# Unread matrix products in PE's queue at eleven places between stages of a two-block transformer kernel

## The chip, the cores and the metric

The kernel runs on one core of a Trainium2 chip. The metric is the device time of one execution in microseconds (us). The core's engines work side by side, each from a queue of its own: PE multiplies matrices (its weight loads are listed as PEld), DVE, ACT and POOL do the element-wise work, SP starts most transfers. PE's clock has two levels, 1.2 and 2.4 GHz; the profile shows the level that was granted as 0.50 or 1.00.

## The reference

Two transformer blocks run one after the other, each with two layers, on 512 latent tokens and 256 context tokens of width 1024 in f32. Cut to what matters here:

```
for l in range(2):                       # first block
    a = rmsnorm(h) * (1 + sc1) + sh1
    y = even_mixer(a) if l == 0 else odd_mixer(a)   # attention; output projection inside
    h = h + g1 * y
    h = h + g2 * swiglu(rmsnorm(h) * (1 + sc2) + sh2)
x = rmsnorm(h)
for i in range(2):                       # second block
    y = rwkv_pool_mixer(..) if i == 0 else na_mixer(..)
    x = layer_norm(alpha * x + g_m * y)
    x = layer_norm(alpha * x + g_f * swiglu(x * (1 + sc_f) + sh_f))
```

Each normalisation needs the mean of squares of a token over all 1024 features, and so all the output chunks of the stage before it.

## The kernel before

The residual `h` lies transposed in eight chunks of 128 features (partitions) by up to 768 tokens. A product of f32 accuracy is made of three passes (`mm3`): weights and inputs are split into a high and a low part, and high x high (L306), high x low (L308) and low x high (L310) are added in one PSUM tile (`pd` or `sc`). Weights come by SP's transfers; ACT makes the high part (L298), POOL the low one (L299). Inputs are split in the same way (ACT L509, DVE or POOL L510).

Between two stages stands a statistic, `Stat`. For each output chunk DVE adds the gated result to the residual (L574), ACT squares it, and DVE sums the squares (L181). When the last chunk is in, `finish` adds over the partitions with eight tiny PE products (L195), DVE makes the reciprocal root in a chain of small operations (`st_r`, L446 last), and PE spreads it over the partitions by f32 products of 128x128 with the identity (L453, `bcast`); with layer_norm the mean `st_m` goes the same way. Then chunk by chunk DVE normalises (L557, L558), ACT scales, and the parts are split; these are the inputs of the next stage's passes.

`by_parts` makes the last chunks of a stage in two halves of the tokens, so that the first half's statistic (`next(norm)`) runs beside the second half's passes; then `Fill(norm).drain()` does the rest. `out_proj` and `out_late` (second block, behind rwkv) and the feed-forward's last group (`ffn`) end in it. In `out_late` the context tokens are a third part, whose statistic comes ahead of these two. The mixers `even_mixer` and `odd_mixer` begin with a `prep`: the first projections, copies to SBUF by ACT (keys `ks`, values `vs`), rotary embedding on DVE and POOL, transposes of the values (`token_major`, L748), scores (L861 in the even mixer, L1085 in the odd one), softmax on DVE and ACT.

All this is written in program order, and a scheduler puts it into one queue for each engine; PE takes its queue in that order. The small PSUM tiles are named `pq`, of which there are two buffers.

Of the kernel before, what the change touches and what calls it, by code (L numbers as in the profile page):

```python
# [21 lines left out]
P = 128  # L22
D = 1024
KC = 8
NL = 512
NC_ = 256
T = NL + NC_
# [3 lines left out]
LAST = 3  # L31
# [112 lines left out]
class Stat:  # L144
# [44 lines left out]
    def finish_(self, x, z):  # L189
# [10 lines left out]
        if self.mean:  # L200
            m = k.small("st_m", 8)[:, :nb]
            q = k.small("st_q", 8)[:, :nb]
            nc.vector.tensor_scalar(m, ps[:, 8:8 + nb], 1.0 / D, None, op0=ALU.mult)
            nc.vector.tensor_tensor(out=q, in0=m, in1=m, op=ALU.mult)
            nc.vector.scalar_tensor_tensor(v, v, EPS, q, op0=ALU.add, op1=ALU.subtract)
        k.rsqrt(r, v, nb)
        if self.rt:
# [10 lines left out]
class Kern:  # L218
# [65 lines left out]
    def segs(n):  # L284
        return [(0, 512, 0)] + ([(512, n, 512)] if n > 512 else [])


    def wload(self, src, lo_eng=None):
# [243 lines left out]

    def ln_modulated(self, out, h, n, st, lname, m, sh, sc, scale, dst=None, parts=None):

# [15 lines left out]
        for y, z in parts:  # L550
            st.finish(y, z)
            if (y, z) != parts[-1]:
                yield
            r = int(y >= NL)
            for k in range(KC):
# [19 lines left out]

    def by_parts(self, ws, x, n, done, norm):

        for a, b in self.parts(n):
            for i, hl in ws:
                ps = self.pd()  # L580
                for kc in range(len(hl)):
                    self.mm3(ps, *hl[kc], x[0][kc], x[1][kc], kc == 0, kc == len(hl) - 1, [(a, b, a)])
                done(i, ps, a, b)
            if a == 0:
                next(norm, None)
        Fill(norm).drain()

# [5 lines left out]

    def out_proj(self, w, y, order, load, m, g, n, h, st, norm):

        with self.tc.tile_pool(name=self.nm("ylo"), bufs=6, reuse_waits="tile") as yp:
            self.out_proj_(w, y, order, load, m, g, n, h, st, norm, yp)

    def out_proj_(self, w, y, order, load, m, g, n, h, st, norm, yp):
        nc = self.nc  # L600
# [15 lines left out]
        for k in range(2, KC - LAST):  # L616
            done(k, self.chunk(w[k], y, n), 0, n)
        self.by_parts([(k, self.wload(w[k])) for k in range(KC - LAST, KC)], y, n, done, norm)

# [10 lines left out]

    def ffn(self, x, wg, wu, wo, h, m, g, n, st, norm, fill, parts):

# [10 lines left out]
        def down(gi, hid):  # L643
# [34 lines left out]
            if last:  # L678
                self.by_parts(late, xs, n, done, norm)

# [70 lines left out]
    def even_mixer(self, x, first):  # L751
# [8 lines left out]
        def prep(h):  # L760
# [8 lines left out]
            psk = psk or self.chunk(w[12 + h], x, T)  # L769
            nc.scalar.copy(ks, psk[:, :T])  # L770
            self.rope(ks)
            k1, klo = self.stack_k(ks, T)
# [160 lines left out]

    def values(self, ps):

# [4 lines left out]
        for pt, a, b in self.token_major(vs):  # L940
            nc.scalar.copy(v[:, a:b], pt)
        return v.rearrange("p (b d) -> p b d", d=P)

# [86 lines left out]
    def odd_mixer(self, x):  # L1030
# [19 lines left out]
        def prep(c):  # L1050
            kc = c // 4
            if c % 4 == 0:
# [3 lines left out]
                psk = psk or self.chunk(w[8 + kc], x, T)  # L1056
                nc.scalar.copy(ks, psk[:, :T])
                self.rope(ks)
                for s in range(2):
# [7 lines left out]
                yield  # L1067
                v = self.values(psv or self.chunk(w[10 + kc], x, T))
                kv[2 * kc] += (v,)
# [86 lines left out]

    def ffn_block(self, a, win, wout, l, h, m, g, n, st, norm, fill=None, parts=None):
        wi, wo = self.I[win], self.I[wout]
        self.ffn(a, lambda c: wi[l * 44 + c], lambda c: wi[l * 44 + 22 + c], lambda c: wo[l * 22 + c], h, m, g, n, st, norm, fill or Fill(), parts)

# [11 lines left out]
    def layer0(self):  # L1172
# [4 lines left out]
        with ExitStack() as es:  # L1177
# [9 lines left out]
            norm = self.rms_modulated(a, h, T, st, "norm2_g0", m, 24, 32)  # L1187
            self.out_proj(I["even_w_out"], y, [4, 5, 6, 7, 0, 1, 2, 3], load, m, 16, T, h, st, norm)
            self.dump("hm0", h, T)
        with ExitStack() as es:  # L1190
# [3 lines left out]
            norm = self.rms_modulated(b, h, T, st, "norm1_g1", job[0], 0, 8)  # L1194
            self.ffn_block(a, "ffn_w_in", "ffn_w_out", 0, h, m, 40, T, st, norm, Fill(self.ada(job, range(6))))
        self.dump("h0", h, T)
        return h, b, job

    def layer1(self, h, a, job):
        I = self.I  # L1200
        m = job[0]
        with ExitStack() as es:
# [6 lines left out]
            norm = self.rms_modulated(a, h, NL, st, "norm2_g1", m, 24, 32)  # L1209
            self.out_proj(I["odd_w_out"], y, list(range(KC)), self.load([(self.spd, 0, NL, None)]), m, 16, NL, h, st, norm)  # L1210
            self.dump("hm1", h, NL)
# [411 lines left out]
    def out_late(self, h, st, m, norm):  # L1623
# [10 lines left out]
        for k in range(KC - LAST):  # L1634
# [7 lines left out]
            if k == NORMAT:  # L1642
                next(norm)
        self.by_parts([(k, wl(k)) for k in range(KC - LAST, KC)], xs, NL, done, norm)

# [237 lines left out]
    def second(self, h, st, job):  # L1883
# [3 lines left out]
        with self.es2 as es0:  # L1887
# [9 lines left out]
            with ExitStack() as es:  # L1897
# [4 lines left out]
                st, b = self.stat(T, True), self.pairs()  # L1902
                norm = self.ln_modulated(b, h, T, st, "01", job[0], 0, 8, ALPHA)
                self.ffn_block(a, "ffn_w13", "ffn_w2", 0, h, m, 40, T, st, norm, Fill(self.ada(job, range(6))), parts)
            m = job[0]
            with ExitStack() as es:
# [8 lines left out]
                norm = self.ln_modulated(a, h, NL, st, "10", m, 24, 32, ALPHA)  # L1915
                self.out_proj(I["od_w_out"], y, list(range(KC)), self.load([(self.spd, 0, NL, None)]), m, 16, NL, h, st, norm)
                self.dump("xm1", h, NL)
# [215 lines left out]
```

## Time and profile before

| | |
|---|---|
| median of 3 runs | 4023.65 us (4017.19 to 4030.66) |
| the profiled execution | 4027.45 us, of which 4025.6 are the span from first to last instruction |
| mean granted clock of PE | 0.943 |
| PE busy | 3673.8 us, 91% of the span |
| DVE, ACT, POOL busy | 2253.0, 1347.9, 1348.5 us (56%, 33%, 33%) |

Busy shares are means over stages with different limits; what a place between stages is worth is read from the timeline there: what PE waits for, how long, and what it does next. In the rows that are shown further down, the value in square brackets is the idle time of the engine before the instruction, with what ended it. A row `x4` stands for four records in a row; an f32 product of 128x128 makes two of them. Matmuls overlap, so that the price of one is the distance between starts rather than its own length.

### The profile page before, as it was taken

The numbers are of one execution on the slowest core, as the hardware profiler recorded it, in microseconds if no ns is written. First come the engines' busy times: TensorE is split into PE (matmuls) and PEld (weight loads), VectorE is DVE, ScalarE is ACT, GpSimd is POOL, SyncE is SP. The second block draws the span as 40 slices with busy tenths as digits, with TensorE's granted clock in tenths as the row PEclk, the third lists the DMA queues.
The fourth block names the chain that finished last, engine by engine and source line by source line (L and its number), as shares of the span: only waits on it lengthen the run. The fifth ranks groups of instructions, "written<-read, shape, count | busy, mean of one in ns | idle before, by whom it ended". The sixth has DMA issues, their size and how long they took to land. (4 is left out here: it accounts for less than half of the span.)

```text
span 4025.6 us, 57375 instructions
## 1 busy us (share of the span) xinstructions
PE 3673.8 (91%) x22809; PEld 3183.3 (79%) x22809; DVE 2253.0 (56%) x4289; ACT 1347.9 (33%) x2337; POOL 1348.5 (33%) x798
## 2 busy tenths in 40 slices
PE   6989999999789899999877879699999899989997
PEld 4777799999677778877765667599999777778886
DVE  4884554333776677746777564755444654364225
ACT  5542212112466222234333222331111365543223
POOL 2112332222312444432221125552222542245443
PEclk9999999999899999989987779899999899999998
DMA  5124133333101255424445677223334222122331
GB/s 195 38 90 158 56 110 126 121 119 117 49 27 53 89 176 175 158 82 127 128 138 175 200 204 265 82 64 122 119 121 127 72 63 64 57 74 79 100 95 58
DMA packets 263003, 450.19 MB, mean 112 GB/s; under 512 B 63504, under 2 KB 168592, under 8 KB 259664
## 3 DMA queue, kind: packets, MB, share of 16 engines
q1 hardware_dynamic: 257536, 424.50, 33.6%
q10 hardware_dynamic: 5200, 22.02, 1.7%
q8 instruction: 180, 2.95, 0.3%
q14 instruction: 87, 0.71, 0.1%
HBM read 383.02 MB, written 63.44 MB: 111 GB/s over the span
## 5 line engine op out<-in xcount | busy, mean ns | idle before, releaser
L299 POOL TENSOR_TENSOR wlo<-wraw,whi 128x1024 fp32r<-128x1024 f32 (+2 forms) x406 | 941.5, 2321 | 1944.0 <-ACT whi L298 1820.2
L306 PE MATMUL pd<-s,whi 128*128 128x384 f32 (+2 forms) x3481 | 1050.7, 354 | 38.1 <-ACT s L509 9.5
L310 PE MATMUL pd<-s,wlo 128*128 128x384 f32 (+2 forms) x3481 | 1045.0, 351 | 1.6 <-POOL wlo L299 1.6
L308 PE MATMUL pd<-s,whi 128*128 128x384 f32 (+2 forms) x3421 | 1034.0, 352 | 12.3 <-DVE s L510 5.2
L298 ACT CAST whi<-wraw 128x1024 fp32r<-128x1024 f32 (+2 forms) x414 | 406.0, 982 | 1589.9 <-PE pd L308 899.6
L306 PEld LDWEIGHTS pd<-s,whi 128*128 128x128 f32 x3481 | 630.9, 191 | 104.7 <-issue 14.6
L308 PEld LDWEIGHTS pd<-s,whi 128*128 128x128 f32 x3421 | 622.3, 191 | 69.8 <-DVE s L510 7.6
L310 PEld LDWEIGHTS pd<-s,wlo 128*128 128x128 f32 x3481 | 632.1, 191 | 56.2 <-POOL wlo L299 3.5
L372 DVE SCALAR_TENSOR_TENSOR junk<-wraw,cond 128x1024 bf16<-128x1024 f32 x160 | 275.3, 1721 | 383.9 <-DMA wraw<-in_ada_w 383.7
L574 DVE SCALAR_TENSOR_TENSOR h<-pd,mod,h 128x256 f32<-128x256 f32 (+3 forms) x407 | 206.3, 547 | 187.7 <-PE pd L310 186.2
L696 DVE TENSOR_TENSOR s<-s,pd 128x768 f32<-128x768 f32 (+1 forms) x80 | 65.3, 817 | 289.2 <-PE pd L310 283.2
L306 PE MATMUL pd<-hid,whi 128*128 128x384 f32 (+2 forms) x624 | 192.7, 346 | 4.7 <-DVE h L574 4.2
L308 PE MATMUL pd<-hid,whi 128*128 128x384 f32 (+2 forms) x624 | 191.6, 344 | 0.9 <-DVE hid L335 0.9
L310 PE MATMUL pd<-hid,wlo 128*128 128x384 f32 (+2 forms) x624 | 191.0, 343 | 0.0
L966 DVE TENSOR_REDUCE negm<-sc 128x1 f32<-128x512 f32 (+1 forms) x128 | 96.2, 754 | 117.1 <-PE sc L1147 106.1
L372 DVE SCALAR_TENSOR_TENSOR wraw<-wraw,cond 128x1024 f32<-128x1024 f32 x96 | 133.2, 1388 | 4.0
L306 PEld LDWEIGHTS pd<-hid,whi 128*128 128x128 f32 x624 | 117.7, 192 | 15.8 <-DVE h L574 2.4
L306 PE MATMUL pd<-in,whi 128*128 128x256 f32 (+1 forms) x384 | 113.4, 362 | 14.4 <-DVE h L1240 12.4
L308 PEld LDWEIGHTS pd<-hid,whi 128*128 128x128 f32 x624 | 117.7, 192 | 9.7 <-DVE hid L335 1.3
L310 PEld LDWEIGHTS pd<-hid,wlo 128*128 128x128 f32 x624 | 117.7, 192 | 8.2
L181 DVE TENSOR_TENSOR s<-s,s 128x256 f32<-128x256 f32 (+2 forms) x106 | 101.7, 960 | 36.6 <-ACT s L180 35.0
L308 PE MATMUL pd<-in,whi 128*128 128x256 f32 (+1 forms) x384 | 115.0, 366 | 2.9 <-POOL in L510 1.9
(377 smaller groups left out, 5717.9 us busy)
## 6 DMA issues: line engine op xcount, KB each, us to landing
wraw<-in_ada_w SPq DMA_DIRECT2D x160, 512.0 KB, 3.5
wraw<-in_ffn_w SPq DMA_DIRECT2D x132, 512.0 KB, 3.6
wraw<-in_ffn_w_in SPq DMA_DIRECT2D x88, 512.0 KB, 3.6
wraw<-in_ffn_w_out SPq DMA_DIRECT2D x44, 512.0 KB, 3.5
recd<-xr SPq DMA_DIRECT2D x72, 256.0 KB, 2.9
rec<-recd ACTq DMA_DIRECT2D x12, 1536.0 KB, 7.3
rec<-recd SPq DMA_DIRECT2D x12, 1536.0 KB, 7.0
raw<-in_ada_w SPq DMA_DIRECT2D x32, 512.0 KB, 5.8
```

Of the source, the lines that this page charges most:

```text
L181: nc.vector.tensor_tensor(out=self.sq[:, a:b], in0=self.sq[:, a:b], in1=t[:, a:b], op=ALU.add)
L298: nc.scalar.copy(hi, raw)
L299: (lo_eng or nc.gpsimd).tensor_tensor(out=lo, in0=raw, in1=hi.bitcast(F32), op=ALU.subtract)
L306: nc.tensor.matmul(ps[:, o:o + b - a], lhsT=whi, rhs=xhi[:, a:b], start=start, stop=False)
L308: nc.tensor.matmul(ps[:, o:o + b - a], lhsT=whi, rhs=xlo[:, a:b], start=False, stop=False)
L310: nc.tensor.matmul(ps[:, o:o + b - a], lhsT=wlo, rhs=xhi[:, a:b], start=False, stop=stop)
L372: nc.vector.scalar_tensor_tensor(raw if r else self.junk, raw, 1.0, self.cond[r], op0=ALU.mult, op1=ALU.mult, accum_out=m[:, j, r:r + 1])
L574: nc.vector.scalar_tensor_tensor(h[k][:, x:y], ps[:, x - o:y - o], m[:, g + k, r:r + 1], h[k][:, x:y], op0=ALU.mult, op1=ALU.add)
L696: nc.vector.tensor_tensor(out=cut(sl), in0=cut(sl), in1=bank(pu), op=ALU.mult)
L966: nc.vector.tensor_reduce(nm, ps[:, base:T], axis=AX.X, op=ALU.max, negate=True)
```

## The change

A new function issues n products of the ones matrix with 128 columns of a tile into one `pq` tile; nothing reads it. Eleven places call it, with 16 to 50 products, 311 in all. Signatures on the way gain an argument. The diff, cut to its core:

```
+    def warm(self, x, n):
+        if n:
+            ps = self.pq()[:, :P]
+            for _ in range(n):
+                self.nc.tensor.matmul(ps, lhsT=self.ones, rhs=x[:, :P], start=True, stop=True)
...
@@ finish_ (st.rt: layer 1's end, ahead of rwkv)
+        if self.rt and z == self.n:
+            k.warm(self.sq[:, x:z], 16)
         k.rsqrt(r, v, nb)
...
@@ ln_modulated
             if (y, z) != parts[-1]:
                 yield
+            if y == parts[0][0]:
+                self.warm(st.r[:, y:z], warm)
...
@@ by_parts
             if a == 0:
                 next(norm, None)
+        if warm:
+            self.warm(h[ws[-1][0]][:, a:b], warm)
         Fill(norm).drain()
...
@@ even_mixer, prep
             nc.scalar.copy(ks, psk[:, :T])
+            if h == 0:
+                self.warm(ks[:, NL:], 35)
             self.rope(ks)
...
@@ values
         for pt, a, b in self.token_major(vs):
             nc.scalar.copy(v[:, a:b], pt)
+        self.warm(vs, warm)
...
@@ odd_mixer, prep
                 nc.scalar.copy(ks, psk[:, :T])
+                if c == 0:
+                    self.warm(ks[:, NL:], 25)
                 self.rope(ks)
...
-                v = self.values(psv or self.chunk(w[10 + kc], x, T))
+                v = self.values(psv or self.chunk(w[10 + kc], x, T), 0 if c else 35)
...
@@ the numbers for by_parts: first block's out_proj 20 and 20, its first feed-forward 20;
@@ second block: out_late, first feed-forward, out_proj
-        self.by_parts([(k, wl(k)) for k in range(KC - LAST, KC)], xs, NL, done, norm)
+        self.by_parts([(k, wl(k)) for k in range(KC - LAST, KC)], xs, NL, done, norm, h, 50)
...
-                norm = self.ln_modulated(b, h, T, st, "01", job[0], 0, 8, ALPHA)
+                norm = self.ln_modulated(b, h, T, st, "01", job[0], 0, 8, ALPHA, warm=35)
...
-                self.ffn_block(a, "ffn_w13", "ffn_w2", 0, h, m, 40, T, st, norm, Fill(self.ada(job, range(6))), parts)
+                self.ffn_block(a, "ffn_w13", "ffn_w2", 0, h, m, 40, T, st, norm, Fill(self.ada(job, range(6))), parts, 15)
...
-                self.out_proj(I["od_w_out"], y, list(range(KC)), self.load([(self.spd, 0, NL, None)]), m, 16, NL, h, st, norm)
+                self.out_proj(I["od_w_out"], y, list(range(KC)), self.load([(self.spd, 0, NL, None)]), m, 16, NL, h, st, norm, 40)
```

Line numbers of the changed file are some 9 to 18 higher: the products are its L295, L306/L308/L310 become L315/L317/L319, L453 becomes L462. Three places in PE's queue follow, each before and changed.

PE's queue behind `out_late`, before: the second statistic's sums and spreading, the first passes of the feed-forward (`pd_2278x`), the third sums.

```order
L195 MATMUL pq_22532<-ones_79,s_22216 128x1 x2
L195 MATMUL pq_22532<-ones_79,s_22218 128x1 x2
L453 MATMUL pq_22532<-ident_72,st_r_22538 128x128 x2
L453 MATMUL pq_22563<-ident_72,st_m_22540 128x128 x2
L306 MATMUL pd_22784<-s_22472,whi_22768 128x256
L308 MATMUL pd_22784<-s_22473,whi_22768 128x256
L310 MATMUL pd_22784<-s_22472,wlo_22769 128x256
...
L306 MATMUL pd_22786<-s_22480,whi_22780 128x256
L195 MATMUL pq_22663<-ones_79,s_22216 128x1 x2
L195 MATMUL pq_22663<-ones_79,s_22218 128x1 x2
L308 MATMUL pd_22786<-s_22481,whi_22780 128x256
```

The same place now.

```order
L195 MATMUL pq_22710<-ones_79,s_22394 128x1 x2
L195 MATMUL pq_22710<-ones_79,s_22396 128x1 x2
L462 MATMUL pq_22710<-ident_72,st_r_22716 128x128 x2
L462 MATMUL pq_22741<-ident_72,st_m_22718 128x128 x2
L295 MATMUL pq_22793<-h_21207,ones_79 128x128 x8
L195 MATMUL pq_22892<-ones_79,s_22394 128x1 x2
L195 MATMUL pq_22892<-ones_79,s_22396 128x1 x2
L295 MATMUL pq_22793<-h_21207,ones_79 128x128 x26
L462 MATMUL pq_22892<-ident_72,st_r_22898 128x128 x2
L295 MATMUL pq_22793<-h_21207,ones_79 128x128 x3
L462 MATMUL pq_22923<-ident_72,st_m_22900 128x128 x2
L295 MATMUL pq_22793<-h_21207,ones_79 128x128 x13
L315 MATMUL pd_23013<-s_22650,whi_22997 128x256
```

The 50 products have four places around the last statistic, and the feed-forward's first pass, which stood ahead of the third sums and of the third spreading, stands behind the last product. Of the 64 passes that stood ahead of the third spreading none is left there.

PE's queue at the end of block 2's first feed-forward, before: the context's spreading, the mixer's first passes, the last sums (39 passes in all stand ahead of the last spreading).

```order
L453 MATMUL pq_26957<-ident_72,st_r_26967 128x128 x4
L453 MATMUL pq_26994<-ident_72,st_m_26969 128x128 x4
L306 MATMUL pd_27312<-s_27118,whi_27296 128x512
L306 MATMUL sc_27313<-s_27118,whi_27302 128x512
L306 MATMUL sc_27314<-s_27118,whi_27308 128x512
L308 MATMUL pd_27312<-s_27119,whi_27296 128x512
L195 MATMUL pq_27178<-ones_79,s_26787 128x1 x2
L195 MATMUL pq_27178<-ones_79,s_26789 128x1 x2
L310 MATMUL pd_27312<-s_27118,wlo_27297 128x512
L308 MATMUL sc_27313<-s_27119,whi_27302 128x512
```

The same place now, down to the first half of the last spreading.

```order
L295 MATMUL pq_27343<-h_21207,ones_79 128x128 x15
L295 MATMUL pq_27359<-s_27017,ones_79 128x128 x13
L195 MATMUL pq_27459<-ones_79,s_27016 128x1 x2
L195 MATMUL pq_27459<-ones_79,s_27018 128x1 x2
L295 MATMUL pq_27359<-s_27017,ones_79 128x128 x22
L315 MATMUL pd_27593<-s_27399,whi_27577 128x512
...
L315 MATMUL sc_27595<-s_27407,whi_27589 128x512
L462 MATMUL pq_27459<-ident_72,st_r_27465 128x128 x2
```

28 products stand ahead of the last sums, 22 behind them, and of the mixer's passes 16 are left ahead of the last spreading; the three that stood ahead of the sums now follow them.

PE's queue at the odd mixer's entry, before: the last of 24 query passes (`pd_8605`), the transposes of the values, the first scores.

```order
L306 MATMUL pd_8605<-s_8302,whi_8601 128x512
L308 MATMUL pd_8605<-s_8303,whi_8601 128x512
L310 MATMUL pd_8605<-s_8302,wlo_8602 128x512
L748 MATMUL pq_8556<-ident_72,s_8553 128x128 x3
L748 MATMUL pq_8561<-ident_72,s_8553 128x128 x3
L1085 MATMUL sc_8580<-s_8541,s_8573 128x256 x2
L1048 MATMUL sc_8580<-msk_8385,identr_77 128x128
L1085 MATMUL sc_8580<-s_8542,s_8573 128x256 x2
```

The same place now: keys copied, 25 products, and so on.

```order
L295 MATMUL pq_8614<-s_8612,ones_79 128x128 x25
L315 MATMUL pd_8745<-s_8331,whi_8741 128x512
L761 MATMUL pq_8660<-ident_72,s_8657 128x128 x3
L761 MATMUL pq_8665<-ident_72,s_8657 128x128 x3
L317 MATMUL pd_8745<-s_8332,whi_8741 128x512
L295 MATMUL pq_8670<-s_8657,ones_79 128x128 x35
L1103 MATMUL sc_8720<-s_8645,s_8713 128x256 x2
L1064 MATMUL sc_8720<-msk_8463,identr_77 128x128
L1103 MATMUL sc_8720<-s_8646,s_8713 128x256 x2
L319 MATMUL pd_8745<-s_8331,wlo_8742 128x512
```

Only two of the 24 query passes (now `pd_8745`) are left ahead of the first scores; 25 products stand ahead of the transposes and 35 behind them.

## Rows read from the trace of the kernel before

**Rows 1.** The page's busy times, share of the span, instructions.

```profile
PE 3673.8 (91%) x22809; PEld 3183.3 (79%) x22809; DVE 2253.0 (56%) x4289; ACT 1347.9 (33%) x2337; POOL 1348.5 (33%) x798
```

**Rows 2.** Windows: stretch, us, PE busy (count), granted clock, DMA share, GB/s.

```profile
87.40:107.90 20.50, 16.23 (x44) 0.50 0.09 26
459.40:466.30 6.90, 6.40 (x18) 0.51 0.23 76
1070.40:1087.50 17.10, 8.43 (x31) 0.50 0.11 32
2603.00:2626.90 23.90, 11.00 (x56) 0.57 0.12 39
3193.50:3214.00 20.50, 11.40 (x37) 0.50 0.36 118
3613.40:3627.00 13.60, 7.75 (x35) 0.50 0.23 76
2700.00:2800.00 100.00, 100.00 (x579) 1.00 0.36 116
```

**Rows 3.** PE's timeline behind out_late: start, us, instruction, [idle before <- releaser].

```profile
2608.19 1.87 PE L195 MATMUL pq<-ones,s 128*128 128x1 f32 x8 [9.75 <-DVE s L181]
2616.68 1.22 PE L453 MATMUL pq<-ident,st_r 128*128 128x128 f32 x4 [6.61 <-DVE st_r L446]
2617.77 1.19 PE L453 MATMUL pq<-ident,st_m 128*128 128x128 f32 x4
2618.61 0.56 PE L306 MATMUL pd<-s,whi 128*128 128x256 f32 x1
...
2622.50 1.05 PE L195 MATMUL pq<-ones,s 128*128 128x1 f32 x8 [1.09 <-DVE s L181]
...
2631.20 0.71 PE L453 MATMUL pq<-ident,st_r 128*128 128x128 f32 x4 [0.29 <-DVE st_r L446]
...
2651.60 0.62 PE L306 MATMUL pd<-s,whi 128*128 128x512 f32 x2 [1.01 <-ACT s L691]
```

**Rows 4.** Windows of the passes into pd tiles alone, columns as in 2.

```profile
2618.60:2631.20 12.60, 10.29 (x64) 0.81 0.00 1
2632.10:2650.80 18.70, 18.48 (x152) 1.00 0.00 1
3620.90:3644.90 24.00, 21.57 (x144) 0.87 0.01 2
```

**Rows 5.** PE's timeline behind the second block's od out_proj.

```profile
3619.25 1.87 PE L195 MATMUL pq<-ones,s 128*128 128x1 f32 x8 [7.87 <-DVE s L181]
...
3628.06 0.61 PE L453 MATMUL pq<-ident,st_r 128*128 128x128 f32 x4
3628.51 0.61 PE L453 MATMUL pq<-ident,st_m 128*128 128x128 f32 x4
...
3646.83 0.50 PE L306 MATMUL pd<-s,whi 128*128 128x512 f32 x1 [2.21 <-ACT s L691]
```

**Rows 6.** PE's timeline at the end of block 2's first feed-forward.

```profile
3202.60 0.80 PE L306 MATMUL pd<-s,whi 128*128 128x512 f32 x1 [6.87 <-ACT s L509]
...
3207.07 1.70 PE L195 MATMUL pq<-ones,s 128*128 128x1 f32 x8
...
3223.10 0.71 PE L453 MATMUL pq<-ident,st_r 128*128 128x128 f32 x4 [2.91 <-DVE st_r L446]
```

**Rows 7.** PE's timeline at the odd mixer's entry.

```profile
1071.09 1.54 PE L748 MATMUL pq<-ident,s 128*128 128x128 f32 x6 [4.78 <-ACT s L938]
1078.54 0.77 PE L1085 MATMUL sc<-s,s 128*128 128x256 f32 x2 [5.90 <-DVE s L723]
```

**Rows 8.** Timeline of ACT and PE at the even mixer's entry.

```profile
82.72 0.80 ACT L770 COPY s<-sc 128x768 f32<-128x768 f32 x1
...
90.11 0.79 PE L861 MATMUL sc<-s,s 128*128 128x512 f32 x1 [6.36 <-ACT s L737]
```

**Rows 9.** PE's timeline behind block 1's first out_proj.

```profile
460.06 1.65 PE L306 MATMUL pd<-s,whi 128*128 128x512 f32 x3 [0.50 <-ACT s L509]
```

More of the change, by code (lines that the diff above doesn't have):

```diff
@@ L205, in finish_ @@
             nc.vector.scalar_tensor_tensor(v, v, EPS, q, op0=ALU.add, op1=ALU.subtract)
+        if self.rt and z == self.n:
+            k.warm(self.sq[:, x:z], 16)
         k.rsqrt(r, v, nb)
@@ L285, in segs, with warm @@
         return [(0, 512, 0)] + ([(512, n, 512)] if n > 512 else [])
+    def warm(self, x, n):
+        if n:
+            ps = self.pq()[:, :P]
+            for _ in range(n):
+                self.nc.tensor.matmul(ps, lhsT=self.ones, rhs=x[:, :P], start=True, stop=True)
     def wload(self, src, lo_eng=None):
@@ L531, in rms_modulated, with ln_modulated @@
                 self.split_part(out, k, a, x, y)
-    def ln_modulated(self, out, h, n, st, lname, m, sh, sc, scale, dst=None, parts=None):
+    def ln_modulated(self, out, h, n, st, lname, m, sh, sc, scale, dst=None, parts=None, warm=0):
         nc = self.nc
@@ L574, in residual_add, with by_parts @@
                 nc.vector.scalar_tensor_tensor(h[k][:, x:y], ps[:, x - o:y - o], m[:, g + k, r:r + 1], h[k][:, x:y], op0=ALU.mult, op1=ALU.add)
-    def by_parts(self, ws, x, n, done, norm):
+    def by_parts(self, ws, x, n, done, norm, h=None, warm=0):
         for a, b in self.parts(n):
@@ L617, in out_proj_ @@
             done(k, self.chunk(w[k], y, n), 0, n)
-        self.by_parts([(k, self.wload(w[k])) for k in range(KC - LAST, KC)], y, n, done, norm)
+        self.by_parts([(k, self.wload(w[k])) for k in range(KC - LAST, KC)], y, n, done, norm, h, warm)
     def load(self, srcs):
@@ L629, in load, with ffn @@
         return f
[L631 removed]
+    def ffn(self, x, wg, wu, wo, h, m, g, n, st, norm, fill, parts, warm):
         nc = self.nc
@@ L678, in down @@
             if last:
-                self.by_parts(late, xs, n, done, norm)
+                self.by_parts(late, xs, n, done, norm, h, warm)
         before = None
@@ L932, in lam, with values @@
         return lam
-    def values(self, ps):
+    def values(self, ps, warm=0):
         nc = self.nc
@@ L1067, in prep @@
                 yield
-                v = self.values(psv or self.chunk(w[10 + kc], x, T))
+                v = self.values(psv or self.chunk(w[10 + kc], x, T), 0 if c else 35)
                 kv[2 * kc] += (v,)
@@ L1209, in layer1 @@
             norm = self.rms_modulated(a, h, NL, st, "norm2_g1", m, 24, 32)
-            self.out_proj(I["odd_w_out"], y, list(range(KC)), self.load([(self.spd, 0, NL, None)]), m, 16, NL, h, st, norm)
+            self.out_proj(I["odd_w_out"], y, list(range(KC)), self.load([(self.spd, 0, NL, None)]), m, 16, NL, h, st, norm, 20)
             self.dump("hm1", h, NL)
@@ L1643, in out_late @@
                 next(norm)
-        self.by_parts([(k, wl(k)) for k in range(KC - LAST, KC)], xs, NL, done, norm)
+        self.by_parts([(k, wl(k)) for k in range(KC - LAST, KC)], xs, NL, done, norm, h, 50)
     def rw_invert(self, c, xls):
@@ L1915, in second @@
                 norm = self.ln_modulated(a, h, NL, st, "10", m, 24, 32, ALPHA)
-                self.out_proj(I["od_w_out"], y, list(range(KC)), self.load([(self.spd, 0, NL, None)]), m, 16, NL, h, st, norm)
+                self.out_proj(I["od_w_out"], y, list(range(KC)), self.load([(self.spd, 0, NL, None)]), m, 16, NL, h, st, norm, 40)
                 self.dump("xm1", h, NL)
```

27 lines of the change are left out of this document (18 added, 9 removed).

## The prediction

> **What bounds the kernel now.** The page's busy lines come first: TensorE (PE) computes for 3673.8 us of the 4025.6 us span [rows 1]; no other engine comes near. Next come stretches of that engine. Inside a feed-forward it is never idle: 100.00 busy in 100.00 us, granted clock 1.00 [rows 2]. There, whatever is put into its queue, or whatever useful pass is done later, lengthens the kernel one for one. The idle time lies where stages meet: the last chunk of one must be added, squared, summed, normalised and split on DVE, ACT and POOL before the next can start. At those places the granted clock has fallen to 0.50, the lower level of 1.2 GHz (one stretch holds a little more, 0.57): six stretches of 6.9 to 23.9 us each [rows 2], with PE computing in them for 16.23, 6.40, 8.43, 11.00, 11.40 and 7.75 us. So there is something to win: if that work ran at 2.4 GHz it would take half, 61.2 / 2 = 30.6 us less. Whether it is won is read from the timeline: does PE wait there for another engine, or does it already have useful passes to do?
>
> The junction behind out_late has both [rows 3]. PE waits 9.75 us for DVE's sum of squares (L181), makes the sums (L195), waits 6.61 us for the reciprocal root (st_r, L446), and spreads it (L453). But then, from 2618.61 on, it does feed-forward passes on inputs already there, while DVE does the statistics of the last part. The third sums stand at 2622.50, the third L453 is released at 2631.20. By then 64 of the 216 passes of this first group are done; 152 follow [rows 4].
>
> **What one product costs.** The added product (f32, 128x128) doesn't exist in the trace under its own name; L453 has the same shape and type, and is two records per product. Four such records take 0.45 us from 3628.06 to 3628.51 [rows 5], so a product is 0.22 us at the higher clock. At the lower one, 2617.77 to 2618.61 is 0.84 us for four [rows 3], 0.42 a product. The 311 products are thus 68 us of PE time at full clock and 131 at half. What of that lies in waits costs nothing; the rest, and passes pushed behind it, does.
>
> **Where the products stand.** The order of PE's queue shows that they aren't all in waits.
>
> Out_late, 50 products. None stands in the 9.75 us, none in the 6.61 us: the first 8 come behind the second L453, 26 behind the third L195, 3 and 13 around the third L453, and only then the first feed-forward pass. The first 34 fill DVE's statistics, 2618.6 to 2631.2: 8 x 0.42 = 3.4 us, up to the sums at 2622.50, then 26 x 0.22 = 5.7 us, done by about 2629 to 2631. So r goes out at 2631.20 as before, then 0.45, 3 products 0.66, m 0.45, 13 products 2.86: passes start near 2635.6. All 216 are still to do, at 0.12 us each (152 in 18.48 [rows 4]): 25.9 us, so 2661.5. Before, the group ended at 2650.6 (2651.60 less its idle 1.01 [rows 3]). Late by 10.9. The idle of 1.01 could take as much back. Even if the root came at once, 42 products behind the sums of 2622.50 (1.05 us) end at 2632.8, passes at 2658.7: +8, less 1 is 7. I take **+10, bounds +7 and +11**. Behind it PE is dense, so nothing returns it.
>
> Block 2, first feed-forward's end, 15 + 35 products. 28 fall into the wait of 6.87 us [rows 6]; that hides them (28 x 0.22 = 6.2 us; at 0.42, 11.8, still short of the sums near 3207). The other 22 stand behind L195 (ended near 3208.8): to 3213.6 or, slow, 3218. Then the order has 16 passes ahead of the last L453, where before it had 39. The L453 itself waits for DVE until 3223.10. So 23 passes of 512 columns (twice the 0.12 of 256, an estimate: 0.24) move behind it: 5.5 us. Waits of the mixer that follows may return some: **+4, bounds 0 and +6**.
>
> Second block's od out_proj, 40 products. The first 5 fill a little of the 7.87 us idle; 20 stand behind the sums (end near 3621.1): to 3625.5 or 3629.6. Then r, 3, m, 12 (0.45 + 0.66 + 0.45 + 2.64 = 4.2): passes start between 3629.7 and 3633.8, 144 of them [rows 4] x 0.12 = 17.3: 3647.0 to 3651.1, where before they ended at 3644.6 (3646.83 less 2.21 [rows 5]). **+4, bounds +2 and +7.** Its cold stretch is already in this: the passes that ran there at half rate are now counted at full rate.
>
> Odd mixer's entry, 25 + 35. Before, PE used the wait for 24 useful passes, idled 4.78, transposed at 1071.09, idled 5.90, and scored at 1078.54 [rows 7]. Now 25 products take the passes' place (23 passes, 5.5 us, go behind the first scores) and 35 stand behind the transposes: started near 1073.1, mixed clock, until about 1081 to 1083. Scores start 2 to 4 later; against this stands half of 8.43 busy at the lower clock, 4.2, and softmax waits. **+2.5, bounds 0 and +6.**
>
> Even mixer's entry, 35. They start when ACT's copy of the keys is done, near 83.5, where PE waited 6.36 us for the first scores at 90.11 [rows 8]; 35 take 7.7 us, so 91.2, past these; and the values' transposes now stand ahead of these scores, some 2 us more. Half of 16.23 busy, 8.1, is on the other side, but of it only what DVE's softmax lets through. **0, bounds -4 and +4.**
>
> The two out_proj and the feed-forward of block 1 (20 each) and the 16 before rwkv: 14 or 15 products follow the last sums, 3.1 to 6.3 us, where PE waited 0.50 before its first pass (460.06 [rows 9]); what the lower clock cost there, 6.40 / 2 = 3.2, comes back. Together **+1, bounds -3 and +6.** New waits are few: the products of out_proj wait for the last residual sum, and nothing but PE's own queue waits behind them. DVE, ACT and POOL keep their work; SP's queue is the same, so no transfer moves.
>
> Sum: 10 + 4 + 4 + 2.5 + 0 + 1 = 21.5 us (bounds +2 and +40). The profiled execution took 4027.45 us, 3.8 above the median of 4023.65; on the median this gives **4045 us**, own range 4025 (bound +2) to 4063 (+40).
>
> **The clock, rule against row.** After the two idles of 9.75 and 6.61 us four records take 0.84 us, where the same four take 0.45 behind a run of passes [rows 3, 5], and the six stretches lie at such places: the trace shows that waiting costs clock. The Trainium skill, "TensorE: Matmul & The Clock Gate", section "Why this matters for your kernels", says the same and advises to leave no long PE-idle gaps between bursts of matmuls; by that alone the sum would be -30.6 us, 3993. My sum goes by the queue's order instead, since at the costliest place the products don't stand in the two long idles but ahead of useful passes.
>
> **Rivals.**
> 1. Faster: the clock gain decides. It needs PE's passes to be limited by rate at the six cold stretches, and the products to end before their stage's release. For it: 61.2 us of work there at half rate. Against it: the push at out_late alone is certain by the order, and needs a third of it. If half of the 30.6 is won beyond the pushes: 4008. It turns where the pushes stay under the gains, that is, where out_late's group ends before 2651. Chance 0.25.
> 2. No change that can be measured (0.3% is 12 us, about what the runs' own spread of 13 us can tell): the pushes shrink to my lower bounds, for later stages have more slack than seen, and the cold stretches return the rest. On the median, with +2, 4026. Chance 0.23.
> 3. Far slower: products run at the lower level throughout, since short f32 products don't lift it; 131 in place of 68 us, some 30 of the extra past the waits. 4070. Against it: 152 passes at 0.12 us follow the half-rate records [rows 3, 4], so the rate comes back while PE works. Chance 0.04, within slower.
>
> Forecast as such: 0.48. Chances: faster 0.25, same 0.23, slower 0.52. The range for 8 in 10 reaches into the first rival and to the upper bound: 4003 to 4063.
>
> **What would show it.** In the changed profile: products at 0.22 us, and these places: the junction behind out_late without a feed-forward pass until 4 us after the third L453, and its group ending 8 to 11 late; at the end of block 2's first feed-forward the same idle before the last L453 and 16 passes ahead of it; scores of the odd mixer 2 to 4 later; granted clock above 0.50 in most of the six stretches. The prediction is wrong if gains of clock inside the mixers exceed 10 us, or if st_r comes much earlier than before.

## The result, and the profile after

The changed kernel takes **4056.86 us** (median of 4 runs, 4050.16 to 4066.0) against 4021.88 for the kernel before in the same comparison (4 runs, 4017.19 to 4030.66): ratio 1.0085, interval 1.0063 to 1.0108. It is some 35 us slower. The forecast was 4045, slower.

The profiled execution took 4050.16 us, with a mean granted clock of 0.953. The line of its page that answers to [rows 1] (busy time, share of the span, instructions of each engine):

```profile
PE 3719.0 (92%) x23431; PEld 3236.6 (80%) x23431; DVE 2253.9 (56%) x4289; ACT 1347.0 (33%) x2337; POOL 1347.2 (33%) x798
```

PE has 622 records more, two for each of the 311 products. DVE, ACT and POOL do what they did, in times that moved by less than 1.4 us. The clock is higher than before (0.953 against 0.943), and the kernel is slower all the same. The windows at the six places of [rows 2], moved to where they lie now and widened to take in the products (stretch, us, PE busy and count, granted clock, DMA share, GB/s):

```profile
84.30:103.00 18.70, 18.68 (x116) 0.91 0.09 29
459.00:466.00 7.00, 7.00 (x42) 0.76 0.21 75
1074.00:1098.00 24.00, 22.07 (x137) 0.93 0.08 23
2603.00:2632.00 29.00, 15.45 (x94) 0.65 0.11 36
3205.00:3236.00 31.00, 21.36 (x143) 0.87 0.35 121
3635.00:3649.00 14.00, 13.04 (x79) 0.66 0.09 36
```

A wider window also takes in more work at the higher level, so these figures do not compare with the 0.50 to 0.57 of [rows 2]. In windows of the same widths at the same places the kernel before has 0.58, 0.53, 0.64, 0.65, 0.67 and 0.59; the rows of out_late and of od out_proj:

```profile
2602.50:2631.50 29.00, 15.31 (x90) 0.65 0.11 36
3615.60:3629.60 14.00, 10.35 (x57) 0.59 0.11 39
```

So the products raise the clock at the two mixers' entries, at block 1's first out_proj and at the end of block 2's first feed-forward, by little at od out_proj (0.59 to 0.66, and 0.63 in the kernel with all counts at zero), and not at all at out_late (0.65 in both). PE's timeline behind out_late shows what the products cost (start, us, instruction, idle before and its releaser; the first row answers to the first of [rows 3]):

```profile
2608.71 1.87 PE L195 MATMUL pq<-ones,s 128*128 128x1 f32 x8 [9.74 <-DVE s L181]
2617.19 1.22 PE L462 MATMUL pq<-ident,st_r 128*128 128x128 f32 x4 [6.61 <-DVE st_r L455]
...
2619.27 2.60 PE L295 MATMUL pq<-h,ones 128*128 128x128 f32 x16
2623.00 1.05 PE L195 MATMUL pq<-ones,s 128*128 128x1 f32 x8 [1.14 <-DVE s L181]
2623.92 7.68 PE L295 MATMUL pq<-h,ones 128*128 128x128 f32 x52
2631.68 0.71 PE L462 MATMUL pq<-ident,st_r 128*128 128x128 f32 x4
...
2633.40 3.07 PE L295 MATMUL pq<-h,ones 128*128 128x128 f32 x26
2636.22 0.36 PE L315 MATMUL pd<-s,whi 128*128 128x256 f32 x1
...
2663.38 0.62 PE L315 MATMUL pd<-s,whi 128*128 128x512 f32 x2 [1.01 <-ACT s L704]
```

Read it from top to bottom. The two long idles are untouched: 9.74 and 6.61 us, where [rows 3] have 9.75 and 6.61. After the second spreading come 8 products instead of feed-forward passes, then 26, 3 and 13 around the third statistic, and the first feed-forward pass starts at 2636.22, where before it started at 2618.61. From the third sums (L195) to the first pass of the next group it is 2663.38 - 2623.00 = 40.38 us, and before 2651.60 - 2622.50 = 29.10 [rows 3]: **11.3 us** lost at this place alone. The spreading itself is not late: it comes 8.68 us behind the third sums, before 8.70. So the products do not hold it up, though their tile is one of the two `pq` buffers; what is late is the passes.

The other two places of the second block, in the same view: the end of block 2's first feed-forward [rows 6], and od out_proj [rows 5].

```profile
3211.41 3.07 PE L295 MATMUL pq<-s,ones 128*128 128x128 f32 x26
3219.01 1.84 PE L195 MATMUL pq<-ones,s 128*128 128x1 f32 x8 [4.54 <-DVE s L181]
...
3235.36 1.22 PE L462 MATMUL pq<-ident,st_r 128*128 128x128 f32 x4 [3.88 <-DVE st_r L455]
...
3257.86 0.62 PE L315 MATMUL pd<-s,whi 128*128 128x512 f32 x2 [1.42 <-ACT s L966]
...
3638.22 1.71 PE L195 MATMUL pq<-ones,s 128*128 128x1 f32 x8
...
3670.57 0.50 PE L315 MATMUL pd<-s,whi 128*128 128x512 f32 x1 [2.21 <-ACT s L704]
```

28 products lie in the wait ahead of the last sums at 3219.01, as the order had it; 22 lie behind them, and PE still waits 3.88 us for st_r (2.91 in [rows 6]): the useful passes that could have run there stand further back. From the sums to the row that the mixer's ACT releases with an idle of 1.42 it is 38.85 us. In the kernel before, that row is

```profile
3240.52 0.61 PE L306 MATMUL pd<-s,whi 128*128 128x512 f32 x2 [1.42 <-ACT s L950]
```

which is 33.45 us behind its sums at 3207.07 [rows 6]: 5.4 lost. (The kernel with all counts at zero, below, has 33.49.) At od out_proj it is 3670.57 - 3638.22 = 32.35 against 27.58 [rows 5]: 4.8 lost.

At the odd mixer's entry, the same view (L761 are the transposes, L748 before; L1103 the scores):

```profile
1074.24 1.46 PE L761 MATMUL pq<-ident,s 128*128 128x128 f32 x6 [4.36 <-ACT s L953]
1075.92 8.87 PE L295 MATMUL pq<-s,ones 128*128 128x128 f32 x70
1084.55 0.48 PE L1103 MATMUL sc<-s,s 128*128 128x256 f32 x2
...
1098.54 0.90 PE L1103 MATMUL sc<-s,s 128*128 128x384 f32 x2 [2.23 <-ACT s L987]
```

Transposes to first scores: 10.31 us, against 7.45 [rows 7]. The 35 products (8.63 us from start to start) are longer than the idle of 5.90 that they fill. The later scores at 1098.54 come 24.30 us behind the transposes; before, they came 19.49 behind:

```profile
1090.58 0.45 PE L1085 MATMUL sc<-s,s 128*128 128x384 f32 x2
```

So the delay is not given back there: it has grown from 2.9 to 4.8 us.

### The profile page after: what moved, and what is told of

Same layout as the page of the kernel before. It is cut to its first block, busy times and chain, and to the rows that moved or that the text cites. A ratio compares the mean times of both kernels' runs of the same rounds, so it can differ in the third digit from the quotient of the medians.

```text
span 4048.4 us, 58631 instructions
## 1 busy us (share of the span) xinstructions
PE 3719.0 (92%) x23431; PEld 3236.6 (80%) x23431; DVE 2253.9 (56%) x4289; ACT 1347.0 (33%) x2337; POOL 1347.2 (33%) x798
## 4 chain that ended last, share of the span: by engine, by line
PE 41%; DVE 9%; DMA 2%; issue 2%; ACT 2%; POOL 0%; SPq 0%; DVEq 0%; ACTq 0%; POOLq 0%
PE pd L315 10%; PE pd L319 9%; PE pd L317 9%; PE pq L1010 1%; DMA recd<-xr 1%; DVE s L181 1%; DVE h L171 1%; PE ch L1786 1%; PE sc L1165 1%; PE c L1543 1%; DVE lf L1691 1%; DVE itmp L1689 1%; PE ch L1773 1%; PE pq L1025 1%; PE b L1422 1%
## 5 line engine op out<-in xcount | busy, mean ns | idle before, releaser
L308 POOL TENSOR_TENSOR wlo<-wraw,whi 128x1024 fp32r<-128x1024 f32 (+2 forms) x406 | 940.8, 2319 | 1977.4 <-ACT whi L307 1880.3
L315 PE MATMUL pd<-s,whi 128*128 128x384 f32 (+2 forms) x3481 | 1051.3, 352 | 29.1 <-ACT s L704 7.9
L319 PE MATMUL pd<-s,wlo 128*128 128x384 f32 (+2 forms) x3481 | 1043.1, 350 | 1.6 <-POOL wlo L308 1.6
L317 PE MATMUL pd<-s,whi 128*128 128x384 f32 (+2 forms) x3421 | 1028.9, 351 | 6.3 <-DVE s L344 3.8
L315 PEld LDWEIGHTS pd<-s,whi 128*128 128x128 f32 x3481 | 629.2, 190 | 94.1 <-issue 14.2
L319 PEld LDWEIGHTS pd<-s,wlo 128*128 128x128 f32 x3481 | 628.7, 190 | 56.8 <-POOL wlo L308 3.5
L317 PEld LDWEIGHTS pd<-s,whi 128*128 128x128 f32 x3421 | 618.6, 190 | 59.3 <-DVE s L344 4.4
L315 PE MATMUL pd<-hid,whi 128*128 128x384 f32 (+2 forms) x624 | 193.3, 347 | 4.7 <-DVE h L585 4.2
L317 PE MATMUL pd<-hid,whi 128*128 128x384 f32 (+2 forms) x624 | 192.1, 345 | 1.5 <-DVE hid L344 1.5
L319 PE MATMUL pd<-hid,wlo 128*128 128x384 f32 (+2 forms) x624 | 191.6, 344 | 0.0
L315 PEld LDWEIGHTS pd<-hid,whi 128*128 128x128 f32 x624 | 118.3, 193 | 15.7 <-DVE h L585 2.4
L317 PEld LDWEIGHTS pd<-hid,whi 128*128 128x128 f32 x624 | 118.3, 193 | 10.1 <-DVE hid L344 1.9
L315 PE MATMUL pd<-in,whi 128*128 128x256 f32 (+1 forms) x384 | 112.3, 359 | 14.9 <-DVE h L1258 12.9
L319 PEld LDWEIGHTS pd<-hid,wlo 128*128 128x128 f32 x624 | 118.2, 193 | 8.2
L317 PE MATMUL pd<-in,whi 128*128 128x256 f32 (+1 forms) x384 | 112.4, 359 | 3.5 <-POOL in L519 1.9
```

What stands on the lines that cost most here:

```text
L308: (lo_eng or nc.gpsimd).tensor_tensor(out=lo, in0=raw, in1=hi.bitcast(F32), op=ALU.subtract)
L315: nc.tensor.matmul(ps[:, o:o + b - a], lhsT=whi, rhs=xhi[:, a:b], start=start, stop=False)
L317: nc.tensor.matmul(ps[:, o:o + b - a], lhsT=whi, rhs=xlo[:, a:b], start=False, stop=False)
L319: nc.tensor.matmul(ps[:, o:o + b - a], lhsT=wlo, rhs=xhi[:, a:b], start=False, stop=stop)
```

## The experiments

The theory to be tested: products delay useful passes in PE's queue at the second block's places and the odd mixer, and a higher clock returns little of it. The rivals: the time is lost to something else (the scheduler's new order or buffers), or the clock does return time, and other products placed in true waits would win. Each kernel is the changed one with other counts. "All other counts" means those of the eleven that the diff does not name; they are set to 0. The three groups of kernels ran on three occasions, each with its own runs of the kernel before (medians 4021.9, 4026.93 and 4023.57 us). An expectation is told as it was recorded.

### Control: the same code with no products, all eleven counts at 0

```diff
-            k.warm(self.sq[:, x:z], 16)
+            k.warm(self.sq[:, x:z], 0)
...
-                    self.warm(ks[:, NL:], 25)
+                    self.warm(ks[:, NL:], 0)
...
-        self.by_parts([(k, wl(k)) for k in range(KC - LAST, KC)], xs, NL, done, norm, h, 50)
+        self.by_parts([(k, wl(k)) for k in range(KC - LAST, KC)], xs, NL, done, norm, h, 0)
```

> The changed code with every count at zero: PE's order is that of before, row for row. A control: the ratio to before is 1 within what repeated runs scatter, and its profile gives the stretch of rwkv, 1850 to 2490 us, which no product touches, a second time. If that stretch is 6 to 10 us shorter than in the profile of before, as in the five other profiles, it was the profile of before that was long there; if not, the products shorten it.

Measured: 4030.66 us, ratio 1.0007 (0.9996 to 1.0019). PE's timeline behind out_late, the third sums:

```profile
2625.28 1.05 PE L195 MATMUL pq<-ones,s 128*128 128x1 f32 x8 [1.07 <-DVE s L181]
```

The group's release, with idle 1.01, is at 2654.36: 29.08 us behind the sums, as before (29.10). Without products there is nothing left of the loss, so it comes with the products, and not with the changed signatures. Of the later ratios, a few hundredths of a per cent are no effect. The question about the stretch of rwkv got neither of the two answers: it is 3.9 us shorter than in the profile of before (1850 to 2490 us, by the starts of ACT's instructions), and 1.0 to 13.5 us shorter in the other profiles, with and without products ahead of it. It varies by itself (last section).

### The change once more

```diff
 (the changed kernel, no edit)
```

> The changed kernel once more, for a narrower interval and a second profile. Theory: the losses at the places repeat in the profile within 0.5 us (out_late 11.3 from the third sums to the next group, block 2's feed-forward end and out_proj 5 to 6 each), while the stretches that no product touches differ by up to 10 us from one execution to the next; the time is 30 to 36 us above before.

Measured: 4059.28 us (5 runs, 4047.99 to 4066.41), ratio 1.0085 (1.0071 to 1.0099). Out_late repeats, 40.39 us from sums to release, and so does od out_proj, 32.03 (4.5 lost). Block 2's first feed-forward doesn't repeat within the 0.5 us expected: 37.38 (3.9 lost, and not 5.4). The difference lies behind the last spreading, where the same 112 records take 19.60 us at a granted clock of 1.00 here and 21.00 at 0.93 in the first profile: among dense passes the clock was worth 1.4 us. Transposes to first scores are 11.05 (3.6 lost).

### out_late alone, with 50 and with 34 products

```diff
         self.by_parts([(k, wl(k)) for k in range(KC - LAST, KC)], xs, NL, done, norm, h, 50)
 (all other counts 0)
...
-        self.by_parts([(k, wl(k)) for k in range(KC - LAST, KC)], xs, NL, done, norm, h, 50)
+        self.by_parts([(k, wl(k)) for k in range(KC - LAST, KC)], xs, NL, done, norm, h, 34)
 (the second kernel; all other counts 0)
```

With 50:

> Only the 50 products behind out_late are left; the other ten places have none. Theory (order of PE's queue): all of this place's loss remains, the feed-forward's first group behind out_late ends 11 us later than before counted from the same instruction ahead of it (changed kernel: 11.1), and the kernel takes 11 us more than before. Rival (the clock decides, the products pay back where they raise it): the group ends less than 3 us late, the whole within 3 us of before.

With 34:

> Only out_late, with 34 products in place of 50. These 34 all lie in front of the third spreading, in time in which DVE makes the statistic; but the 64 useful passes still stand behind it. Theory (displaced passes): the first group ends 64 x 0.12 = 7.7 us late. Rival (only the products that stick out of the waits cost): 0 to 1 us. With the 50 of before, 11.1 = 7.7 + 16 x 0.22.

Measured: 50 products 4037.68 us, 1.0041 (1.0025 to 1.0056); 34 products 4037.26 us, 1.0029 (1.0015 to 1.0043). PE's timeline of the kernel with 50, then of the one with 34:

```profile
2616.79 1.05 PE L195 MATMUL pq<-ones,s 128*128 128x1 f32 x8 [0.87 <-DVE s L181]
2617.70 6.05 PE L295 MATMUL pq<-h,ones 128*128 128x128 f32 x52
2625.46 0.71 PE L462 MATMUL pq<-ident,st_r 128*128 128x128 f32 x4 [1.71 <-DVE st_r L455]
...
2657.17 0.62 PE L315 MATMUL pd<-s,whi 128*128 128x512 f32 x2 [1.01 <-ACT s L704]
```

```profile
2623.46 1.05 PE L195 MATMUL pq<-ones,s 128*128 128x1 f32 x8 [1.16 <-DVE s L181]
2624.38 7.68 PE L295 MATMUL pq<-h,ones 128*128 128x128 f32 x52
...
2660.22 0.62 PE L315 MATMUL pd<-s,whi 128*128 128x512 f32 x2 [1.01 <-ACT s L704]
```

With 50 alone: 40.38 us from sums to release, as in the whole change. With 34: 36.76, 7.7 us lost. That is 64 passes x 0.12 = 7.7, to the tenth, though all 34 products lie in time in which DVE was making the third statistic. The remaining 3.6 belong to the 16 products around and behind the third spreading (16 x 0.22 = 3.5). Both terms of the step are seen one by one. In the first fence the 26 products run faster (6.05 us) than in the second (7.68), and PE waits 1.71 us for DVE instead of not at all: the release is the same. What PE gains there, it waits. By the runs' times the 50 cost 10 to 23 us (0.0025 to 0.0056 of 4022), which holds the 11 expected and leaves out the rival's 3; the 34 cost 6 to 17.

### Products inside the 6.6 us idle, at the same place

```diff
+        if getattr(k, 'root', 0):
+            k.warm(self.sq[:, x:z], k.root)
+            k.root = 0
...
         k.rsqrt(r, v, nb)
@@ by_parts
             if a == 0:
+                self.root = early
                 next(norm, None)
 (out_late: early 16; all counts 0)
```

> No product anywhere but 16 behind out_late, placed between the sums and the spreading of the second statistic, that is wholly inside the idle of 6.6 us; the feed-forward's first passes keep their place of before. Theory: the passes between 2618 and 2631 run at the higher level and are done 2 to 3 us earlier, but the third spreading still waits for DVE's root, PE idles those 2 to 3 us, and the group ends within 0.7 us of before. Rival (clock decides): the group ends 2 to 4 us earlier than before.

Measured: one run of 4026.53 us, within the spread of the kernel before (4009.36 to 4033.95 in that comparison). PE's timeline (here L465 is the spreading, L298 the products):

```profile
2608.80 5.34 PE L298 MATMUL pq<-s,ones 128*128 128x128 f32 x32
2615.56 0.71 PE L465 MATMUL pq<-ident,st_r 128*128 128x128 f32 x4 [1.41 <-DVE st_r L458]
...
2622.07 1.05 PE L195 MATMUL pq<-ones,s 128*128 128x1 f32 x8 [1.15 <-DVE s L181]
...
2631.08 0.71 PE L465 MATMUL pq<-ident,st_r 128*128 128x128 f32 x4 [2.34 <-DVE st_r L458]
...
2651.41 0.62 PE L318 MATMUL pd<-s,whi 128*128 128x512 f32 x2 [1.01 <-ACT s L708]
```

and the window of the passes between the two spreadings, with the granted clock (in the kernel before, 2617.00 to 2631.20, it is 0.77):

```profile
2616.00:2631.00 15.00, 11.32 (x92) 1.00 0.01 1
```

16 products now fill the 6.6 us, and 1.41 of idle are left. The spreading takes 0.71 us instead of 1.22 [rows 3], at the higher level. Then the third root is waited for: 2.34 us, where [rows 3] have 0.29. The release comes 29.34 us behind the third sums (before 29.10), and 44.33 behind the second ones (before 43.41). So even products that displace nothing, and do raise the clock from 0.77 to 1.00, win nothing here: what PE did sooner only brought it to the next wait sooner, and DVE's chain ends it at the same time.

### The second block's other places

```diff
-        self.by_parts([(k, wl(k)) for k in range(KC - LAST, KC)], xs, NL, done, norm, h, 50)
+        self.by_parts([(k, wl(k)) for k in range(KC - LAST, KC)], xs, NL, done, norm, h, 0)
 (15, 35 and 40 stay; all other counts 0)
```

> Only the second block's first feed-forward (15 and 35) and its out_proj (40). Theory: 4 to 6 us late behind each, 10 to 12 us in all, as in the changed kernel (5.8 and 5.9). Rival (clock): under 5 us in all.

Measured: 4037.25 us, 1.0028 (1.0018 to 1.0039). PE's timeline at the end of block 2's first feed-forward:

```profile
3209.97 1.74 PE L195 MATMUL pq<-ones,s 128*128 128x1 f32 x8 [4.10 <-DVE s L181]
...
3248.83 0.61 PE L315 MATMUL pd<-s,whi 128*128 128x512 f32 x2 [1.42 <-ACT s L966]
```

38.86 us, 5.4 more than in the control; od out_proj 32.64, 4.8 more than the control's 27.81. The two are 10.2 us of the 11 that the ratio gives (0.0028 x 4027).

### The odd mixer's entry: both, 25 alone, 35 alone

```diff
-                v = self.values(psv or self.chunk(w[10 + kc], x, T), 0 if c else 35)
+                v = self.values(psv or self.chunk(w[10 + kc], x, T), 0 if c else 0)
 (25 alone; in a second kernel 35 alone: self.warm(ks[:, NL:], 0) for 25; in a third both stay; all other counts 0)
```

Both:

> Only the 25 and 35 products at the odd mixer's entry. Theory (order): first scores 3 us late, the second scores behind the 23 displaced query passes 8 to 9 us late, and this lag stays to the end of the mixer: 7 to 8.5 us, the whole kernel 7 to 8 more than before. Rival as I had put it in the prediction: the returned clock leaves 2.5 us.

25 alone:

> Odd mixer's entry, only the 25 products behind the keys' copy. The 24 query passes are displaced, but 20 of them now stand in the idle ahead of the first scores, and only 3 behind these. Theory (what counts is how many useful passes come to stand ahead of the second scores): the second scores at most 1 us late, the mixer under 1.5 us. Rival (the 25 products cost their 5.9 us): 4 us and more.

35 alone:

> Only the 35 products behind the transposes; the 24 query passes keep their place of before, and the second scores follow the first at once. Theory: first and second scores both about 3 us late (products from 1073 to about 1082 against 1078.5), the mixer 1 to 3 us. With both sets the second scores were 8.3 late alone and 8.8 in the changed kernel less the 2.9 to 3.1 that came from ahead of the entry, so 5.5. Rival (clock returns it): 0 or earlier.

Measured: both 4029.51 us, 1.0027 (1.0012 to 1.0043); 25 alone 4024.34, 0.9996 (0.9983 to 1.0008); 35 alone 4027.44, 1.0003 (0.9994 to 1.0013). PE's timeline with 25 alone, then with 35 alone:

```profile
1073.93 1.54 PE L761 MATMUL pq<-ident,s 128*128 128x128 f32 x6 [4.36 <-ACT s L953]
...
1081.32 0.51 PE L1103 MATMUL sc<-s,s 128*128 128x256 f32 x2 [0.65 <-DVE s L736]
```

```profile
1076.30 1.54 PE L761 MATMUL pq<-ident,s 128*128 128x128 f32 x6 [4.79 <-ACT s L953]
1077.82 10.28 PE L295 MATMUL pq<-s,ones 128*128 128x128 f32 x70
1087.85 0.48 PE L1103 MATMUL sc<-s,s 128*128 128x256 f32 x2
...
1099.51 0.45 PE L1103 MATMUL sc<-s,s 128*128 128x384 f32 x2
```

The 25 push query passes out of their place too, and cost nothing: the passes fall into the idle ahead of the first scores, which shrinks from 5.90 [rows 7] to 0.65 us (20 of the 24 passes stand in it, as expected), and the scores come 7.39 us behind the transposes (before 7.45). The 35 push nothing aside, but take 10.03 us (granted clock 0.77) where the idle was 5.90: scores 11.55 behind the transposes, 4.1 late, and the later scores 23.21 (before 19.49), still 3.7 late. That is more than was expected of the 35. With both, the first scores come 10.00 us behind the transposes (2.6 late, 3 expected), the second ones, behind the displaced query passes, 15.69 (before 8.65: 7.0 late, 8 to 9 expected), and the later ones 24.06 (4.6 late): part of the delay is given back by then. By the runs' times both cost 5 to 17 us (0.0012 to 0.0043 of 4022), and the 35 alone at most 5.

### The small places

```diff
-        self.by_parts([(k, wl(k)) for k in range(KC - LAST, KC)], xs, NL, done, norm, h, 50)
+        self.by_parts([(k, wl(k)) for k in range(KC - LAST, KC)], xs, NL, done, norm, h, 0)
 (16, 35 at the even entry, 20, 20, 20 stay; all other counts 0)
```

> Only the places of block 1 without the odd mixer: the two out_proj and the feed-forward (20 each), the even mixer's entry (35), and 16 ahead of rwkv. Theory: each between -1 and +2 us, the sum of the five 0 to 4 us against before, too small to be told from the scatter of the whole kernel. Rival (products as such cost, 111 x 0.22 = 24 us): 10 us and more.

Measured: 4030.67 us, 1.0008 (0.9993 to 1.0023): not told from the control's 1.0007, and below the 10 us of the rival (1.0025). Nothing is won at the even entry and the first block's junctions, and little lost.

### Products only where PE waits for the last sums

```diff
-        ps = k.pq()
+        ps, k.pre = getattr(k, 'pre', None) or k.pq(), None
...
+            return ps
...
-            self.warm(h[ws[-1][0]][:, a:b], warm)
+            self.pre = self.warm(self.ones, warm)
 (counts 17, 17, 17 for block 1's junctions, 34 for od out_proj; all others 0)
```

The products multiply ones by ones and write the tile of the sums, so that they stand ahead of these sums in the queue and wait for nothing of DVE.

> Products only ahead of the last sums (17, 17, 17 and 34 of them, in the same PSUM tile as the sums, so that none can stand behind these) at the ends of block 1's two out_proj, its first feed-forward, and the second block's od out_proj; no useful pass is displaced. Theory (order is the loss, the clock a gain where PE has no later wait): 1.5 to 3.5 us won at each of the four, 5 to 10 us faster than before in all. Rival (the clock is worth nothing in this kernel): within 2 us of before. Rival (products as such cost): slower by 3 us and more.

Measured: 4028.73 us, 1.0015 (1.0003 to 1.0028). The expected gain isn't there. PE's timeline at od out_proj, with one row of POOL:

```profile
3603.51 7.75 PE L295 MATMUL pq<-ones 128*128 128x128 f32 x68
...
3610.14 4.46 POOL L175 TENSOR_TENSOR s<-s,h 128x256 f32<-128x256 f32 x1 [2.16 <-DVE h L171]
...
3614.65 0.94 PE L195 MATMUL pq<-ones,s 128*128 128x1 f32 x4 [3.00 <-POOL s L175]
3621.61 0.71 PE L463 MATMUL pq<-ident,st_r 128*128 128x128 f32 x4 [0.47 <-DVE st_r L456]
```

The idle of 7.87 us [rows 5] is filled with 34 products, up to the first half of the sums. The second half then waits 3.00 us more, for POOL's L175, which takes 4.46 us in this profile and 0.77 to 2.12 in the twelve others; why is open. Behind this wait the clock is as low as it was before:

```profile
3614.70:3621.60 6.90, 6.43 (x29) 0.51 0.00 0
```

So od out_proj got no higher clock, and this profile can't tell what one would be worth there. From the spreading of the first half's root to the release it is 40.24 us, in the control 39.51. At block 1's three junctions the granted clock did rise (0.77, 1.00 and 1.00 from the sums to the spreading; in the control 0.51, 0.72 and 0.53), and ACT's instructions behind them come only 0 to 0.3 us sooner against the control. The runs' time shows no gain. No version beats the kernel before.

## Why the prediction was right in sign, and short in size

**The order, not the clock, decided.** The step that read PE's queue held at out_late: both long idles untouched, no feed-forward pass until 4.5 us behind the third spreading (2636.22; 2635.6 was worked out), the group late by 11.3, where the working gave 10.9 and the forecast 10. The runs with 34 and with 50 products show its two terms, 7.7 and 3.6, apart. One size was off without effect: the 26 products took 7.68 us and not 5.7, but still ended with the wait for DVE's root.

**What was mis-sized.** The sum was 21.5 us, and 35 were measured. In the local distances of the changed kernel: out_late +11.3 (forecast 10), block 2's first feed-forward +5.4 and +3.9 in its two profiles (forecast 4; the working gave 5.5 before a return was taken off), od out_proj +4.8 and +4.5 (forecast 4), the odd entry +4.8 at the later scores (forecast 2.5). At out_late, at block 2's first feed-forward and at the odd entry I had taken something off for a return, by the clock or by a later wait, and it didn't come or came in part. Matching ACT's instructions one by one with those of before, the lag over the whole odd mixer grows by 7.9 and 6.1 us in the two profiles (by 4.2 in the kernel with the odd entry's products alone), so that this term is the one furthest off. Its step that failed is the subtraction of 4.2 us for work at half rate: the later scores still wait 2.23 us, for ACT. With that, and 2 to 3 us of such lag at the small places, the places hold some 28 to 32 of the 35 us. The runs' times agree: less the control's 0.0007, the ratios of the four kernels with the products of out_late, of the second block's other places, of the odd entry and of the small places add up to 0.0034 + 0.0021 + 0.0020 + 0.0001 = 0.0076, and the whole change has 0.0078. That the range of the forecast held the result owes something to its width, 60 us.

**Rival 1, the clock gain**, had its turning point at 2651 for the end of out_late's group; it ended at 2662.4 (2663.38 less 1.01). The clock did rise at most places, but not at this one. PE's busy time grew by 45.2 us (3719.0 - 3673.8), while the records of the 311 products take 87.33 us: the other work was some 40 us shorter, an estimate. But some 16 of these lie in the stretch of rwkv, which is as short in a kernel without products there (last section), and the products in the true idle of 6.6 us show what can become of the rest: 0.29 us of waiting for DVE turns into 2.34. The Trainium skill, "TensorE: Matmul & The Clock Gate", section "Why this matters for your kernels", advises to leave no long idle gaps on PE between bursts of matmuls. The traces agree that filling a gap can keep the clock up (0.77 to 1.00 behind the filled idle), and they don't bear out that time follows at these places: the next instruction that counts is released by DVE or ACT.

**Rival 2**, no change, needed the lower bounds at the second block's places; they came at the forecast or above, or just under it (3.9 for 4). **Rival 3**, products at the lower level throughout: 13 products behind the third spreading take 2.82 us (2633.40 to 2636.22), 0.22 each, and all 311 take 0.28 on average, so only a part ran at the lower level. It doesn't hold. (Its time was also added up wrongly: 4045 and 30 are 4075, not 4070.) Among the signs named, "the same idle" before the last L453 of block 2's first feed-forward (2.91 us) was found as 3.88, as 2.90 in the second profile, and as 3.24 with that block's products alone. The sign "granted clock above 0.50" says little: in windows as wide as those after, the kernel before has it too.

**Open**: how much of the odd entry's price the mixer passes on (2.9 us at the first scores, 4 to 8 in the lag at the end of it). By the runs' times both counts together cost more than 25 and 35 apart, with intervals that meet only at 5 us; by the traces they don't: the lag over the mixer is 4.2 us with both, 6.3 with the 35 alone and -0.2 with the 25 alone. The runs don't settle it. What a higher clock would be worth at od out_proj is open too.

## What to carry to other kernels

Before filling an engine's wait, read in the order of its queue what already runs there: a filler that pushes useful work behind the wait costs the full length of that work, even if the filler itself ends before the wait does. A higher clock paid here only up to the next instruction that another engine releases, so look whether that release is near (0.29 us of slack here) before counting the gain. A filler is harmless where the work that it pushes aside falls into an idle of its own length, as with the 25 products; the 35 pushed nothing aside, but were longer than the idle that they filled. And compare a clock only in windows of the same width around the same work.

## What the hardware showed unasked

The same stretch of program, with the same instructions and no product in it, varies by 13 us from one profile to another. Between the sums ahead of the rwkv mixer and the sums behind it, the windows of the kernel before, of the changed one and of the one with 25 products read:

```profile
1719.00:2580.00 861.00, 725.49 (x6594) 0.85 0.54 160
```

```profile
1729.60:2580.60 851.00, 713.51 (x6628) 0.87 0.55 162
```

```profile
1725.00:2572.70 847.70, 707.87 (x6594) 0.87 0.55 162
```

The shorter ones have the higher granted clock and less PE busy time. (Of the 34 records more in the second, 32 are the 16 products ahead of rwkv, at its start; without their 3.8 us the other work there is some 16 us shorter than before.) What sets the profiles apart is not shown. These 10 us are most of the reason why the two profiled executions differ by only 22.7 us (4050.16 - 4027.45) where the medians differ by 35. So of a single pair of profiles only distances within one place were used above, apart from the lag over the odd mixer, and that one differs between profiles.

The clock also fell in one execution and not in another behind nearly the same wait: scores behind an idle of 2.23 us take 0.90 us at 1098.54 in the changed kernel, and 0.56 us behind an idle of 2.27 at the same place of the kernel with the odd entry's products alone (start 1098.06). In the second profile of the changed kernel the first two of these scores, behind the same 2.23, take 0.56, and the clock falls right behind them (the next four take 1.38, where the kernel with the odd entry's products alone has 0.80). What set them apart was not tried.
